# One plain fp32 matmul for each product of a decoder trunk, in place of three fp32r matmuls on split operands

## The chip, the cores and the metric

The kernel runs on one core of one Trainium2 chip. The metric is device time in microseconds (us), median over several executions. The kernel before takes 1388.41 us (three runs, 1388.27 to 1388.46). The engines are named as in the profile: PE (TensorE, matmuls), PEld (its weight loads, which have a row of their own), DVE (VectorE), ACT (ScalarE), POOL (GpSimd) and SP (SyncE, which issues nearly all DMAs here). PE takes one operand as weights (stationary, 128 columns) and streams the other through (the moving operand, up to 512 columns); sums over several matmuls build up in a PSUM bank. L159 means line 159 of the kernel before.

## The reference

The computation is a two-layer causal decoder trunk in float32 on 512 tokens of width 1024, with 256 memory tokens. Cut to what matters:

```python
for l in range(DEPTH):                                    # DEPTH = 2
    h = rmsnorm(x, norm_mix_g[l])
    if l % 2 == 0:
        x = x + pool_conv_mixer(h, ...)                   # 1024 -> 1536, pooling + conv, 1024 -> 1024
    else:
        x = x + mla_attention(h, ...)                     # 16 heads, low-rank q (384) and kv (256)
    x = x + memory_cross_attention(rmsnorm(x, ...), rmsnorm(mem, ...), ...)   # 4 heads of 256
    x = x + conv_ffn(rmsnorm(x, ...), ...)
return rmsnorm(x, final_norm_g)

def conv_ffn(h, w_up, conv_w, conv_b, w_down):
    a, g = jnp.split(h @ w_up, 2, axis=-1)                # 1024 -> 2 x 2816
    g = causal_dwconv(g, conv_w) + conv_b                 # 3 taps
    return (jax.nn.silu(g) * a) @ w_down                  # 2816 -> 1024
```

Nearly all arithmetic is in dense products of 128x128 weight tiles with 512 tokens.

## The kernel before, in words

Activations lie transposed, features on the 128 partitions and the 512 tokens along the free axis. So `x` is 8 tiles of 128x512, an MLP product has 22 such tiles, and one product is a 128x128 weight tile times a 128x512 activation tile.

**Split operands.** Each float32 operand is cut into a high part in the type fp32r and a low part that holds the rest (also fp32r). `load_w` (L147) brings a weight tile of up to 128x1024 by DMA into one of four raw buffers (`wr`), casts it on ACT into `wh` (L152) and forms `wl` as the difference on DVE (L153), with raised priority. Activations are split wherever they are made: `Norm.split` (L259, `hh` and `hl`), `split_psum` (L186), `split_sb` (L193), and by hand for the pooled outputs (L654), the latent queries (L925) and the memory tokens (`memory_gain`). `mm3` (L156) then makes a product from three fp32r matmuls into the same PSUM bank: high by high (L157), high by low (L158 or L159), low by high.

**Stages, in program order.** The mixer of layer 0: 12 output tiles of the input projection over 8 tiles of `h`; the first (`opening`, L621) runs while the tiles of `x` arrive; then the depthwise convolution, 31 taps, most of them as DVE operations (L677) interleaved with the keys and values of the memory tokens for both layers (`memory_kv`, L331); then the output projection. The keys for layer 0 (`K_NATIVE`, L340) were already plain fp32 matmuls on raw weights, with a moving operand of 256 columns. Cross-attention (L376): four heads, scores and values by `mm3`, softmax on DVE and ACT. MLP (`ffn`, L466): 44 output tiles of the up projection, gate and convolution on DVE and ACT, then the down projection. The 22 product tiles are taken in groups of 8, 8 and 6 (`FFN_GROUPS`): as soon as a group is there, its part of all 8 output tiles is summed in PSUM and added to `x` on DVE (L514); the last group goes through `residual` (L288), which also feeds the next norm. Layer 1 has latent attention (L889) in place of the mixer; its scores, transposes and values (L1016, L1041, L1053) are plain fp32 matmuls in both kernels, and so are the transposes of the norms, five taps of the convolution (L688) and one mean (L705). The last group of layer 1 is in `finale` (L517): 256 tokens at a time, so that the final norm of the first half runs beside the second.

**What orders the work.** Every engine runs its own instructions in a fixed order, and semaphores join them. The order is made when the kernel is built: a scheduler goes by the order of the program text and may put an instruction earlier where its inputs are there (`tc.high_priority` moves the splits of the weights ahead by 40 places; ACT's diagonal matrices of L687 run during the opening). Where the text interleaves (taps, `filler`, heads of the latent attention with a lag of 2) it was written so by hand. All weight loads go through SP's queue in program order, and a load waits until its raw buffer is free; before, that is when `wl` has been formed. All activations live in a pool of `SLOTS` = 58 tiles of 128x512, and PSUM has 8 banks.

```python
def mm3(ps, ah, al, bh, bl, first, last):
    pe.matmul(ps, ah, bh, start=first, stop=False)
    pe.matmul(ps, ah, bl, start=False, stop=False)
    pe.matmul(ps, al, bh, start=False, stop=last)
```

Of the kernel before, what the change touches and what calls it, by code (L numbers as in the profile page):

```python
# [12 lines left out]
F32R = mybir.dt.float32r  # L13
# [6 lines left out]
P = 128  # L20
# [30 lines left out]
SLOTS = 58  # L51
AHEAD = 40
FIN_AHEAD = 2
K_NATIVE = (True, False)
# [8 lines left out]
FFN_GROUPS = (8, 8, 6)  # L63

# columns of the packed per-channel constants
# [16 lines left out]
def _split_2pi():  # L82
    """2*pi*512 and 2*pi cut into parts whose products with the counts below are exact in float32."""
    def head(v, bits):
        m, e = math.frexp(v)
        return math.ldexp(math.floor(m * 2 ** bits), e - bits)

    big = 2.0 * math.pi * 512.0
    parts = []
    rest = big  # L90
    for _ in range(3):
        h = head(rest, 11)
        parts.append(h)
        rest -= h
    parts.append(rest)
    d1 = head(2.0 * math.pi, 13)
    return parts, (d1, 2.0 * math.pi - d1)
# [3 lines left out]
def kernel(ctx: ExitStack, tc: tile.TileContext, a):  # L101
# [24 lines left out]
    def f(t):  # L126
        return t.bitcast(F32)

# [13 lines left out]
    def load_raw(src, n):  # L142
        raw = wp.tile([P, WCOLS], F32, tag="wr", name=uid("wr"), bufs=4)
        sp.dma_start(raw[:, :n], src)
        return raw

    def load_w(src, n):  # L147
        raw = load_raw(src, n)
        hi = wp.tile([P, WCOLS], F32R, tag="wh", name=uid("wh"), bufs=3)
        lo = wp.tile([P, WCOLS], F32R, tag="wl", name=uid("wl"), bufs=3)  # L150
        with tc.high_priority(offset=AHEAD):
            act.copy(hi[:, :n], raw[:, :n])  # L152
            vec.tensor_tensor(lo[:, :n], raw[:, :n], f(hi[:, :n]), ALU.subtract)  # L153
        return hi, lo

    def mm3(ps, ah, al, bh, bl, first, last):  # L156
        pe.matmul(ps, ah, bh, start=first, stop=False)  # L157
        pe.matmul(ps, ah, bl, start=False, stop=False)  # L158
        pe.matmul(ps, al, bh, start=False, stop=last)  # L159
# [33 lines left out]
    def split_sb(src, name, shape=(P, T)):  # L193
        h = slot(name + "h", F32R, shape)
        l = slot(name + "l", F32R, shape)
        act.copy(h, src)
        vec.tensor_tensor(l, src, f(h), ALU.subtract)  # L197
        return h, l

    def newton_rsqrt(v, n, name):  # L200
        """1/sqrt(v) of a narrow tile."""
# [13 lines left out]
    def col_sums(acc, n=TB):  # L215
        """sums over the partitions of acc, tokens on partitions: [128, n]."""
# [7 lines left out]
    def row_rate(src, n, name):  # L224
        """1/rms of tokens whose features lie along the free axis: [128, n]"""
# [16 lines left out]
    def spread(r, n=TB, name="rb", out=None):  # L242
        """[128, n] with tokens on partitions -> [128, n * 128] with tokens along the free axis."""
# [7 lines left out]
    class Norm:  # L251
        """h = x * gain as hi and lo parts and the running sum of squares, tile by tile."""
# [6 lines left out]
        def split(self, k):  # L259
            if self.gain is not None:  # L260
                g = col(self.gain, self.base + k)
                h = slot("hh", F32R)
                l = slot("hl", F32R)
                act.activation(h, x[k], AF.Identity, scale=g)  # L264
                vec.scalar_tensor_tensor(l, x[k], g, f(h), ALU.mult, ALU.subtract)  # L265
                self.h.append((h, l))
# [36 lines left out]
    class Memory:  # L303
        """the memory tokens, normalised, in two stages"""
# [11 lines left out]
    def memory_gain(layer, memn, mg, mh):  # L316
        for i in range(KD // 2):
            m = slot("mg", shape=(P, 2, MEM))
            h = slot("mh", F32R, (P, 2, MEM))
            l = slot("ml", F32R, (P, 2, MEM))  # L320
# [3 lines left out]
            act.copy(h, m)  # L324
            vec.tensor_tensor(l, m, f(h), ALU.subtract)
            for j in range(2):
                mg.append(m[:, j, :])
                mh.append((h[:, j, :], l[:, j, :]))
            yield

    def memory_kv(layer, mg, mh, keep, native, kt, vt):  # L331
        """keys [d, mem] per head and values [mem, d]; keep takes each out of PSUM; a step per weight tile"""
        for hd in range(HX):
            ps = bank("kx", (P, 2, MEM))
            for j in range(2):
                src = a["xa_wk"][layer, 2 * hd + j]
                if native:
                    w = load_raw(src, D)
                    for k in range(KD):
                        pe.matmul(ps[:, j, :], w[:, k * P:(k + 1) * P], mg[k], start=k == 0, stop=k == KD - 1)  # L340
                else:
                    Linear(src, KD, ps[:, j, :]).run(mh, 0, KD)
                yield
            kt.append(keep(ps, (P, 2, MEM)))
        for half in range(2):
            ps = [bank("vx") for _ in range(MB)]
            for kk in range(KD // 2):
                wh, wl = load_w(a["xa_wv"][layer, half, kk], 2 * T)
                for j in range(2):
                    k = 2 * kk + j  # L350
                    c = slice(j * T, (j + 1) * T)
                    for m in range(MB):
                        h, l = mh[k]
                        s = slice(m * P, (m + 1) * P)
                        mm3(ps[m], h[:, s], l[:, s], wh[:, c], wl[:, c], k == 0, k == KD - 1)
                yield
            for m in range(MB):
                vt[m].append(keep(ps[m], (P, T)))

    def keep_slot(ps, shape):  # L360
        t = slot("kv0", F32, shape)
# [3 lines left out]
    def keep_whole(ps, shape):  # L365
        t = sl.tile(list(shape), F32, tag="kv1", name=uid("kv1"), bufs=8)
        act.copy(t, ps)
        return t

    def split_kv(kv):  # L370
        kt, vt = kv
        return ([split_sb(t, "k", (P, 2, MEM)) for t in kt],
                [[split_sb(t, "v") for t in row] for row in vt])

# [1 line left out]
    def cross_attention(layer, norm, kv, nxt):  # L376
# [4 lines left out]
        def project(hd, j):  # L381
# [3 lines left out]
            q.setdefault(hd, []).append(split_psum(lin.run(norm.h, KD // 2, KD), "q"))  # L385
            yield

        def scores(hd):
            kh, kl = kt[hd]
            mx = small("xmx", [P, TB])  # L390
            sc = []
            for u in range(2):
                ps = bank("sx", (P, 2, MEM))
                for b in range(2):
                    s = slice((2 * u + b) * P, (2 * u + b + 1) * P)
                    for j in range(2):
                        qh, ql = q[hd][j]
                        mm3(ps[:, b, :], qh[:, s], ql[:, s], kh[:, j, :], kl[:, j, :], j == 0, j == 1)
# [20 lines left out]
        def turn(hd):  # L419
            ptr[hd] = []  # L420
            for m in range(MB):
# [3 lines left out]
                ptr[hd].append(split_psum(pt, "pt"))  # L425

        def values(hd):
            for j in range(2):
                ps = bank("pv")
                c0 = (2 * hd + j) * P  # L430
                for m in range(MB):
                    vh, vl = vt[m][c0 // T]
                    c = slice(c0 % T, c0 % T + P)
                    mm3(ps, vh[:, c], vl[:, c], ptr[hd][m][0], ptr[hd][m][1], m == 0, m == MB - 1)
                o.append(split_psum(ps, "o"))
# [30 lines left out]
    def ffn(layer, norm, nxt, extra=None):  # L466
# [9 lines left out]
        def up(i):  # L476
# [15 lines left out]
            prod.append(split_sb(c, "f"))  # L492
# [3 lines left out]
        k0 = 0  # L496
        i = 0
        for n in FFN_GROUPS:
            k1 = k0 + n
            while i < min(k1 + 1, KF):  # L500
                if i == KF - 1 and nxt is None:
                    last = finale(layer, k0, k1 - k0)
                    next(last)
                up(i)
                i += 1
            if k1 == KF and nxt is None:
                last.send(prod[k0:k1])
                return
            for m in range(KD):
                ps = linear(a["ffn_down"][layer, m][:, k0 * P:k1 * P], prod[k0:k1])  # L510
                if k1 == KF:
                    residual(ps, m, nxt)
                else:
                    vec.tensor_tensor(x[m], x[m], ps, ALU.add)  # L514
            k0 = k1

    def finale(layer, k0, nk):  # L517
        """the last products, half of the tokens at a time, and the final norm of each half"""
        half = T // 2
        part = nk // 2  # L520
        w = []

        def weights(m):
            raw = load_raw(a["ffn_down"][layer, m][:, k0 * P:], nk * P)
            hi = [slot("dh", F32R, (P, part * P)) for _ in range(2)]
            lo = [slot("dl", F32R, (P, part * P)) for _ in range(2)]
            for q in range(2):
                c = slice(q * part * P, (q + 1) * part * P)
# [663 lines left out]
```

## Time and profile before

| | |
|---|---|
| median of the runs | 1388.41 us |
| span of the profiled execution | 1386.6 us |
| PE busy | 1371.6 us (99%), 6532 matmul records |
| PE weight loads busy | 1131.2 us (82%) |
| DVE busy | 889.0 us (64%) |
| ACT busy | 599.2 us (43%) |
| granted PE clock, mean | 0.999 |
| DMA | 135.28 MB, mean 98 GB/s |

The span counts from the first to the last instruction of the profiled execution; the timed median is 1.8 us above it. A matmul's record runs from its start to its modelled end, and records in a stream overlap, so the pace of a stream is read from the distance between starts and not from the length of one record. A plain fp32 product shows as two records with two weight loads: the 64 products of L340 stand as 128.

### The profile page before, as it was taken

Reading aid. Unit: us, or ns where it says so; the run is one execution under the profiler, and the core shown is the slowest. Engines: PE = TensorE matmul, PEld = TensorE weight load, DVE = VectorE, ACT = ScalarE, POOL = GpSimd, SP = SyncE. Lnnn points to the kernel's source line nnn. Section 1 sums busy time; section 2 is a strip of 40 time slices with the busy share of each in tenths; the row PEclk is TensorE's granted clock in tenths of the full one; section 3 lists DMA queues with packets and bytes.
Section 4 is the critical chain, followed back from the end, with each engine's and each line's share of the span. In section 5 each row is a group of like instructions: output and inputs, shape, how many; then the busy total and the mean of one; then the engine's idle time right before and its main releaser. Section 6 shows DMA issues by size and latency. Waiting matters only on the chain.

```text
span 1386.6 us, 16884 instructions
## 1 busy us (share of the span) xinstructions
PE 1371.6 (99%) x6532; PEld 1131.2 (82%) x6532; DVE 889.0 (64%) x1535; ACT 599.2 (43%) x976; POOL 6.3 (0%) x17
## 2 busy tenths in 40 slices
PE   8999999999999999999999999999999999999997
PEld 6888978888888888888887776888888888888887
DVE  6999988555685366445669775755566544653565
ACT  6416456443443143223447786644443322332343
POOL 0000000000000000000100000000000000000000
PEclk9999999999999999999999999999999999999999
DMA  9235524113333333333321111321223333233221
GB/s 331 93 106 188 169 91 145 61 56 98 108 97 91 105 93 93 104 91 87 97 83 50 43 46 46 107 76 61 76 91 96 102 92 106 91 93 106 84 84 62
DMA packets 42560, 135.28 MB, mean 98 GB/s; under 512 B 4848, under 2 KB 6512, under 8 KB 42480
## 3 DMA queue, kind: packets, MB, share of 16 engines
q1 hardware_dynamic: 41904, 133.45, 31.0%
q8 instruction: 51, 0.84, 0.2%
q10 hardware_dynamic: 576, 0.76, 0.2%
q14 instruction: 29, 0.24, 0.1%
HBM read 132.09 MB, written 2.10 MB: 97 GB/s over the span
## 4 chain that ended last, share of the span: by engine, by line
PE 90%; DVE 7%; ACT 2%; issue 1%; DMA 0%; SPq 0%; DVEq 0%; ACTq 0%
PE lin L159 24%; PE lin L157 24%; PE lin L158 24%; DVE cv L677 3%; PE s L1016 1%; PE mpv L1053 1%; DVE wl L153 1%; PE t L1041 1%; PE vx L158 1%; PE vx L159 1%; PE fin L157 1%; PE vx L157 1%; PE fin L158 1%; PE fin L159 1%; ACT p L1024 1%
## 5 line engine op out<-in xcount | busy, mean ns | idle before, releaser
L152 ACT CAST wh<-wr 128x1024 fp32r<-128x1024 f32 (+3 forms) x240 | 239.0, 998 | 485.0 <-PE lin L158 338.4
L157 PE MATMUL lin<-hh,wh 128*128 128x512 f32 x976 | 382.4, 392 | 5.9 <-ACT hh L264 5.9
L158 PE MATMUL lin<-hl,wh 128*128 128x512 f32 x976 | 381.1, 391 | 0.0
L159 PE MATMUL lin<-hh,wl 128*128 128x512 f32 x976 | 380.8, 390 | 0.2 <-DVE wl L153 0.2
L153 DVE TENSOR_TENSOR wl<-wr,wh 128x1024 fp32r<-128x1024 f32 (+3 forms) x240 | 276.9, 1155 | 60.4 <-ACT wh L152 58.9
L157 PEld LDWEIGHTS lin<-hh,wh 128*128 128x128 f32 x976 | 183.8, 188 | 43.2 <-ACT hh L264 5.9
L158 PEld LDWEIGHTS lin<-hl,wh 128*128 128x128 f32 x976 | 183.7, 188 | 39.4 <-DVE hl L265 2.1
L159 PEld LDWEIGHTS lin<-hh,wl 128*128 128x128 f32 x976 | 183.7, 188 | 38.7 <-DVE wl L153 0.7
L158 PE MATMUL lin<-fl,wh 128*128 128x512 f32 x304 | 118.4, 389 | 0.0
L159 PE MATMUL lin<-fh,wl 128*128 128x512 f32 x304 | 118.3, 389 | 0.0
L157 PE MATMUL lin<-fh,wh 128*128 128x512 f32 x304 | 118.1, 389 | 0.0
L514 DVE TENSOR_TENSOR x<-x,lin 128x512 f32<-128x512 f32 x32 | 22.0, 688 | 102.8 <-PE lin L159 102.8
L479 DVE TENSOR_TENSOR g<-lin,rb 128x512 f32<-128x512 f32 x44 | 30.4, 690 | 79.2 <-PE lin L159 79.2
L677 DVE SCALAR_TENSOR_TENSOR cv<-a,con,cv 128x509 f32<-128x509 f32 (+25 forms) x115 | 79.5, 728 | 0.1
L490 DVE TENSOR_TENSOR g<-lin,rb 128x512 f32<-128x512 f32 x44 | 30.4, 691 | 71.6 <-PE lin L159 71.4
L158 PEld LDWEIGHTS lin<-fl,wh 128*128 128x128 f32 x304 | 57.1, 188 | 12.1 <-DVE fl L197 0.2
L157 PEld LDWEIGHTS lin<-fh,wh 128*128 128x128 f32 x304 | 57.1, 188 | 11.8
L159 PEld LDWEIGHTS lin<-fh,wl 128*128 128x128 f32 x304 | 57.1, 188 | 11.7
L488 ACT ACTIVATE c<-c 128x512 f32<-128x512 f32 x44 | 27.8, 633 | 82.1 <-DVE c L487 82.1
L289 DVE TENSOR_TENSOR x<-x,lin 128x512 f32<-128x512 f32 x40 | 27.3, 686 | 35.6 <-PE lin L159 35.6
L158 PE MATMUL lin<-ol,wh 128*128 128x512 f32 x128 | 50.1, 391 | 0.0
L159 PE MATMUL lin<-oh,wl 128*128 128x512 f32 x128 | 49.9, 390 | 0.0
(351 smaller groups left out, 2062.4 us busy)
## 6 DMA issues: line engine op xcount, KB each, us to landing
wr<-in_ffn_up SPq DMA_DIRECT2D x88, 512.0 KB, 3.5
wr<-in_ffn_down SPq DMA_DIRECT2D x32, 512.0 KB, 3.5
wr<-in_xa_wk SPq DMA_DIRECT2D x16, 512.0 KB, 3.7
wr<-in_xa_wv SPq DMA_DIRECT2D x16, 512.0 KB, 4.2
wr<-in_xa_wq SPq DMA_DIRECT2D x16, 512.0 KB, 3.6
wr<-in_xa_wo SPq DMA_DIRECT2D x16, 512.0 KB, 3.5
wr<-in_ffn_down SPq DMA_DIRECT2D x16, 384.0 KB, 3.1
wr<-in_pc_in SPq DMA_DIRECT2D x11, 512.0 KB, 6.6
```

The source lines that it names most:

```text
L152: act.copy(hi[:, :n], raw[:, :n])
L153: vec.tensor_tensor(lo[:, :n], raw[:, :n], f(hi[:, :n]), ALU.subtract)
L157: pe.matmul(ps, ah, bh, start=first, stop=False)
L158: pe.matmul(ps, ah, bl, start=False, stop=False)
L159: pe.matmul(ps, al, bh, start=False, stop=last)
L289: vec.tensor_tensor(x[m], x[m], ps, ALU.add)
L479: vec.tensor_tensor(g, gps, rb, ALU.mult)
L488: act.activation(c, c, AF.Silu)
L490: vec.tensor_tensor(g, aps, rb, ALU.mult)
L514: vec.tensor_tensor(x[m], x[m], ps, ALU.add)
L677: vec.scalar_tensor_tensor(cv[i][:, s:], gl[i][:, :T - s], w, cv[i][:, s:], ALU.mult, ALU.add)
L1016: pe.matmul(ps[i], q[:, i * P:(i + 1) * P], k[:, :P * (i + 1)], start=True, stop=True)
```

## The change

Each product becomes one plain fp32 matmul on the operands as they are. `mm3`, `split_psum`, `split_sb`, `split_kv` and all other splits go: no cast on ACT and no difference on DVE for the weights, and one tile in place of two for each activation. `load_w` is the DMA alone, now into ten buffers (`WBUFS`), and a buffer is free when its last matmul has read it. Where a split's high part also moved a result out of PSUM, one ACT copy (`keep`) or one ACT activation stays. The keys for layer 0 and the matmuls that were plain fp32 stay as they are. The down projection of the MLP in layer 0 becomes, for each of the 8 output tiles, one sum over 22 tiles after all 22 have been made, with one `residual` each. In layer 1 `finale` first sums the first 16 tiles for all 8 output tiles (8 additions to `x`), then the last 6 as before; its weights for these come straight into slots by two DMAs for each output tile. `SLOTS` goes from 58 to 50. Comments and docstrings are dropped.

```diff
-SLOTS = 58
-AHEAD = 40
+SLOTS = 50
+WBUFS = 10
...
     def load_w(src, n):
-        raw = load_raw(src, n)
-        hi = wp.tile([P, WCOLS], F32R, tag="wh", name=uid("wh"), bufs=3)
-        lo = wp.tile([P, WCOLS], F32R, tag="wl", name=uid("wl"), bufs=3)
-        with tc.high_priority(offset=AHEAD):
-            act.copy(hi[:, :n], raw[:, :n])
-            vec.tensor_tensor(lo[:, :n], raw[:, :n], f(hi[:, :n]), ALU.subtract)
-        return hi, lo
...
+        w = wp.tile([P, WCOLS], F32, tag="wr", name=uid("wr"), bufs=WBUFS)
+        sp.dma_start(w[:, :n], src)
+        return w
...
             for k in range(k0, k1):
-                hi, lo = self.load(k)
+                w = self.load(k)
                 c = slice(k % KD * P, (k % KD + 1) * P)
-                xh, xl = xs[k]
-                mm3(self.ps, hi[:, c], lo[:, c], xh, xl, k == 0, k == self.nk - 1)
+                pe.matmul(self.ps, w[:, c], xs[k], start=k == 0, stop=k == self.nk - 1)
             return self.ps
...
-    def split_psum(ps, name, shape=(P, T)):
-        h = slot(name + "h", F32R, shape)
-        l = slot(name + "l", F32R, shape)
-        act.copy(h, ps)
-        vec.tensor_tensor(l, ps, f(h), ALU.subtract)
-        return h, l
...
+    def keep(ps, name, shape=(P, T)):
+        t = slot(name, F32, shape)
+        act.copy(t, ps)
+        return t
...
         def split(self, k):
             if self.gain is not None:
-                g = col(self.gain, self.base + k)
-                h = slot("hh", F32R)
-                l = slot("hl", F32R)
-                act.activation(h, x[k], AF.Identity, scale=g)
-                vec.scalar_tensor_tensor(l, x[k], g, f(h), ALU.mult, ALU.subtract)
-                self.h.append((h, l))
+                h = slot("h")
+                act.activation(h, x[k], AF.Identity, scale=col(self.gain, self.base + k))
+                self.h.append(h)
...
             vec.tensor_tensor(c, c, g, ALU.mult)
-            prod.append(split_sb(c, "f"))
+            prod.append(c)
...
+        for i in range(KF):
+            up(i)
+        if nxt is None:
+            finale(layer, prod)
+            return
+        for m in range(KD):
+            residual(linear(a["ffn_down"][layer, m], prod), m, nxt)
...
         def weights(m):
...
+            hold = [slot("dw", F32, (P, part * P)) for _ in range(2)]
+            for q, t in enumerate(hold):
+                c = (k0 + q * part) * P
+                sp.dma_start(t, a["ffn_down"][layer, m][:, c:c + part * P])
+            w.append(hold)
...
+        for m in range(KD):
+            ps = linear(a["ffn_down"][layer, m][:, :k0 * P], prod[:k0])
+            vec.tensor_tensor(x[m], x[m], ps, ALU.add)
+            if m >= KD - FIN_AHEAD:
+                weights(len(w))
...
                 ps = bank("fin")[:, :half]
-                for k in range(nk):
-                    wc = slice(k % part * P, (k % part + 1) * P)
-                    mm3(ps, hi[k // part][:, wc], lo[k // part][:, wc], prod[k][0][:, c], prod[k][1][:, c],
-                        k == 0, k == nk - 1)
+                for k in range(k0, KF):
+                    q, i = divmod(k - k0, part)
+                    pe.matmul(ps, w[m][q][:, i * P:(i + 1) * P], prod[k][:, c], start=k == k0, stop=k == KF - 1)
```

More of the change, by code (lines that the diff above doesn't have):

```diff
@@ L62 @@
 LATE = (1, 4, 1, 3, 1, 4, 1)
-FFN_GROUPS = (8, 8, 6)
 _COLS = {}
@@ L323, in memory_gain, with memory_kv @@
                                scale=col("norm_mem_g", layer * KD + 2 * i + j))
-            act.copy(h, m)
-            vec.tensor_tensor(l, m, f(h), ALU.subtract)
-            for j in range(2):
                 mg.append(m[:, j, :])
-                mh.append((h[:, j, :], l[:, j, :]))
             yield
-    def memory_kv(layer, mg, mh, keep, native, kt, vt):
+    def memory_kv(layer, mg, hold, kt, vt):
         for hd in range(HX):
@@ L335, in memory_kv @@
             for j in range(2):
[L336 to L342, printed above, removed]
+                Linear(a["xa_wk"][layer, 2 * hd + j], KD, ps[:, j, :]).run(mg, 0, KD)
                 yield
-            kt.append(keep(ps, (P, 2, MEM)))
+            kt.append(hold(ps, (P, 2, MEM)))
         for half in range(2):
@@ L347, in memory_kv, with hold_slot, hold_kv @@
             for kk in range(KD // 2):
-                wh, wl = load_w(a["xa_wv"][layer, half, kk], 2 * T)
+                w = load_w(a["xa_wv"][layer, half, kk], 2 * T)
                 for j in range(2):
                     k = 2 * kk + j
-                    c = slice(j * T, (j + 1) * T)
                     for m in range(MB):
-                        h, l = mh[k]
-                        s = slice(m * P, (m + 1) * P)
-                        mm3(ps[m], h[:, s], l[:, s], wh[:, c], wl[:, c], k == 0, k == KD - 1)
+                        pe.matmul(ps[m], mg[k][:, m * P:(m + 1) * P], w[:, j * T:(j + 1) * T],
+                                  start=k == 0, stop=k == KD - 1)
                 yield
             for m in range(MB):
-                vt[m].append(keep(ps[m], (P, T)))
-    def keep_slot(ps, shape):
-        t = slot("kv0", F32, shape)
+                vt[m].append(hold(ps[m], (P, T)))
+    def hold_slot(ps, shape):
+        return keep(ps, "kv0", shape)
+    def hold_kv(ps, shape):
+        t = sl.tile(list(shape), F32, tag="kv", name=uid("kv"), bufs=8)
         act.copy(t, ps)
         return t
[L365 to L373, printed above, removed]
     def cross_attention(layer, norm, kv, nxt):
@@ L384, in project @@
             yield
-            q.setdefault(hd, []).append(split_psum(lin.run(norm.h, KD // 2, KD), "q"))
+            q.setdefault(hd, []).append(keep(lin.run(norm.h, KD // 2, KD), "q"))
             yield
         def scores(hd):
-            kh, kl = kt[hd]
             mx = small("xmx", [P, TB])
@@ L396, in scores @@
                     for j in range(2):
-                        qh, ql = q[hd][j]
-                        mm3(ps[:, b, :], qh[:, s], ql[:, s], kh[:, j, :], kl[:, j, :], j == 0, j == 1)
+                        pe.matmul(ps[:, b, :], q[hd][j][:, s], kt[hd][:, j, :], start=j == 0, stop=j == 1)
                 vec.reduce_max(mx[:, 2 * u:2 * u + 2], ps, axis=AX.X)
@@ L431, in values @@
                 for m in range(MB):
[L432 to L435, printed above, removed]
+                    pe.matmul(ps, vt[m][c0 // T][:, c0 % T:c0 % T + P], ptr[hd][m], start=m == 0, stop=m == MB - 1)
+                o.append(keep(ps, "o"))
         def out(m):
@@ L491, in up, with finale @@
             vec.tensor_tensor(c, c, g, ALU.mult)
-            prod.append(split_sb(c, "f"))
+            prod.append(c)
             if i == 2 and extra is not None:
                 extra()
[L496 to L517, printed above, removed]
+        for i in range(KF):
[5 more added lines that the diff above has]
+            residual(linear(a["ffn_down"][layer, m], prod), m, nxt)
+    def finale(layer, prod):
         half = T // 2
-        part = nk // 2
+        k0 = 2 * KD
+        part = (KF - k0) // 2
         w = []
         def weights(m):
[L524 to L528, printed above, removed]
-                act.copy(hi[q], raw[:, c])
-                vec.tensor_tensor(lo[q], raw[:, c], f(hi[q]), ALU.subtract)
-            w.append((hi, lo))
+            hold = [slot("dw", F32, (P, part * P)) for _ in range(2)]
[3 more added lines that the diff above has]
+            w.append(hold)
         def final_rate(acc):
@@ L574, in finale @@
         xg = []
-        for m in range(FIN_AHEAD):
-            weights(m)
-        prod = yield
+        for m in range(KD):
[3 more added lines that the diff above has]
+                weights(len(w))
         done = None
@@ L630, in opening @@
                 c = slice(k % half * P, (k % half + 1) * P)
-                mm3(ps, hi[:, c], lo[:, c], *norm.h[k], k == 0, k == KD - 1)
+                pe.matmul(ps, w[:, c], norm.h[k], start=k == 0, stop=k == KD - 1)
             return ps
@@ L652, in pooled @@
             c = slice(i * P, (i + 1) * P)
-            mm3(ps, wh[:, c], wl[:, c], *part, True, True)
-            yh = slot("yah", F32R)
-            yl = slot("yal", F32R)
-            g = col("pool_scale", i)
-            act.activation(yh, ps, AF.Identity, scale=g)
-            vec.scalar_tensor_tensor(yl, ps, g, f(yh), ALU.mult, ALU.subtract)
-            cat.append((yh, yl))
+            pe.matmul(ps, wpool[:, c], part, start=True, stop=True)
+            y = slot("ya")
+            act.activation(y, ps, AF.Identity, scale=col("pool_scale", i))
+            cat.append(y)
         def convolve():
@@ L721, in normalise @@
                 act.activation(cv[i], cv[i], AF.Silu, bias=col("conv_ln_b", i), scale=col("conv_ln_g", i))
-            yield
-            for i in range(CT):
-                cat.append(split_sb(cv[i], "yb"))
+                cat.append(cv[i])
         cv = [sl.tile([P, T], F32, tag="cv", name=uid("cv"), bufs=CT) for _ in range(CT)]
@@ L801, in filler @@
         def filler():
-            for _ in memory_kv(1, *scaled, keep_whole, K_NATIVE[1], *kv):
+            for _ in memory_kv(1, scaled, hold_kv, *kv):
                 yield 2
@@ L831, in mixer @@
             pass
-        out[0] = split_kv(out[0])
         for m in range(KD):
@@ L971, in contents @@
                     c = slice((i * nk + k) * P, (i * nk + k + 1) * P)
-                    mm3(ps, wh[:, c], wl[:, c], xs[k][0], xs[k][1], k == 0, k == nk - 1)
+                    pe.matmul(ps, w[:, c], xs[k], start=k == 0, stop=k == nk - 1)
                 r0, r1 = KIND[k0][0], KIND[k1][0]
@@ L997, in group_values @@
                         c = slice(512 + k * 256, 512 + (k + 1) * 256)
-                        mm3(ps[:, b, :], ckv[k][0][:, s], ckv[k][1][:, s], wh[:, c], wl[:, c],
-                            k == 0, k == KKV - 1)
+                        pe.matmul(ps[:, b, :], ckv[k][:, s], w[:, c], start=k == 0, stop=k == KKV - 1)
                 t = slot("v", F32, (P, 2, 4 * VH))
```

76 lines of the change are left out of this document (24 added, 52 removed).

## The prediction

> **What bounds the kernel now.** I read the page first, its engine lines and slices.
>
> ```profile
> span 1386.6 us, 16884 instructions
> PE 1371.6 (99%) x6532; PEld 1131.2 (82%) x6532; DVE 889.0 (64%) x1535; ACT 599.2 (43%) x976; POOL 6.3 (0%) x17
> PE   8999999999999999999999999999999999999997
> PEclk9999999999999999999999999999999999999999
> ```
>
> PE is busy for 1371.6 of 1386.6 us, in every slice but the first and the last, at a clock granted in full. Busy alone doesn't prove a bound, because records overlap and their ends are modelled. So I went on to the waits of PE, and to stretches where another engine might set the pace.
>
> ```profile
> PE lin L157 <- ACT hh L264: 5.9, 1, 5.9
> PE lin L159 <- DVE wl L153: 0.2, 1, 0.2
> ```
>
> ```profile
> 50.00:100.00 50.00, 50.00 (x219) 40.95 (x218) 50.00 (x96) 11.63 (x21) 0.00 (x0) 1.00 0.29 89
> 400.00:500.00 100.00, 100.00 (x442) 82.82 (x442) 50.90 (x61) 29.60 (x35) 0.00 (x0) 1.00 0.32 95
> 742.00:848.00 106.00, 105.11 (x568) 75.19 (x568) 83.14 (x266) 82.98 (x196) 0.00 (x0) 1.00 0.18 55
> 1350.00:1386.60 36.60, 29.14 (x245) 28.77 (x243) 20.19 (x56) 13.74 (x32) 0.00 (x0) 0.94 0.19 65
> ```
>
> (Columns of the windows: busy time of PE, PEld, DVE, ACT and POOL with their instruction counts, then granted clock, DMA share, GB/s.) PE waits 5.9 us for its first operand and hardly at all after that. In the convolution (50 to 100 us) DVE is full as well, but PE doesn't fall idle beside it; in the MLP (400 to 500) DVE has half its time free; the latent attention (742 to 848) costs PE 0.9 us of idle. The kernel is bound by PE throughout, so the question is what one product costs PE before and after. What goes from DVE and ACT was on nobody's path.
>
> **The pace of three fp32r matmuls.** The timeline of PE in layer 0's MLP and norms gives the start of every matmul; here are the first and the last of 39, all of one kind.
>
> ```profile
> 699.84 0.39 PE L157 MATMUL lin<-hh,wh 128*128 128x512 f32 x1
> ...
> 708.45 0.39 PE L159 MATMUL lin<-hh,wl 128*128 128x512 f32 x1
> ```
>
> 38 steps in 8.61 us: 0.2266 us each, so a product of 512 columns takes 3 x 0.2266 = 0.680 us. With 256 columns, in the last stage (33 records, 32 steps, in 3.84 us):
>
> ```profile
> 1345.05 0.28 PE L159 MATMUL fin<-fh,dl 128*128 128x256 f32 x1
> ...
> 1348.89 0.28 PE L158 MATMUL fin<-fl,dh 128*128 128x256 f32 x1
> ```
>
> 0.120 us each, 0.360 us a product.
>
> **The pace of one plain fp32 matmul.** The kernel has this kind already: 64 products in the keys of layer 0 with 256 columns (128 records, so a product is two), and a few with 512.
>
> ```profile
> 81.67 2.75 PE L340 MATMUL kx<-mg,wr 128*128 128x256 f32 x12
> ```
>
> ```profile
> 180.11 0.86 PE mean L705 x2
> 784.30 2.16 PE s L1016 x8
> ```
>
> ```profile
> L340 PE MATMUL kx<-mg,wr 128*128 128x256 f32 x128 | 28.3, 379 | 0.0
> L1016 PE MATMUL s<-kA,qA 96*128 96x512 f32 x8 | 4.1, 592 | 0.0
> L1016 PE MATMUL s<-kA,qA 96*128 96x256 f32 x8 | 2.4, 379 | 0.0
> ```
>
> The first fence is the timeline, the second the chain of waits, the third groups by shape (busy us, then mean ns of one record). A run of 12 key records spans 2.75 us, the last of them 0.379 long, so 11 steps take 2.371: 0.2155 each, 0.431 us a product of 256 columns, against 0.360 for three fp32r. From 256 to 512 columns a record grows by 592 - 379 = 213 ns. The key record's step of 215.5 ns is thus 213 for its columns and 2.5 fixed, and a 512-column record should step by 426 + 2.5 = 428.5 ns, a product by 0.857 us. Bounds: nothing fixed, 0.852; twice the key product, 0.862. The chain agrees: the mean's two records take 0.86, and a head's eight score records (128, 256, 384 and 512 columns, two each) 2.16, which is 1.69 ns a column or 0.864 for 512. No row shows 512-column products in a long stream; I take 0.857, since the key stream shows the same two-record form held over many products.
>
> So the two-record product is dearer than the three-record one: 0.857 against 0.680. The Trainium skill's "FP8 and Floating Point Precision" (TensorE Precision Notes) speaks against the change too: true fp32 takes four passes through the array. With four times the isolated gap of about 216 ns that "TensorE: Matmul & The Clock Gate" (Back-to-back issue gap) gives for 512 columns, a product would be 0.864 and the added time, as an estimate from these pages, some 11 us more than my sum has. The key stream, 0.431 for 256 columns, agrees with four passes; its own step decides.
>
> **How many products.** The groups by shape give the fp32r records of one of the three lines:
>
> ```profile
> L158 PE MATMUL lin<-hl,wh 128*128 128x512 f32 x976 | 381.1, 391 | 0.0
> L158 PE MATMUL lin<-fl,wh 128*128 128x512 f32 x304 | 118.4, 389 | 0.0
> L158 PE MATMUL lin<-ol,wh 128*128 128x512 f32 x128 | 50.1, 391 | 0.0
> L158 PE MATMUL lin<-mol,wh 128*128 128x512 f32 x64 | 24.9, 390 | 0.0
> L158 PE MATMUL vx<-wl,mh 128*128 128x512 f32 x64 | 25.1, 393 | 0.1
> L158 PE MATMUL fin<-fl,dh 128*128 128x256 f32 x96 | 27.1, 283 | 0.0
> L158 PE MATMUL kx<-ml,wh 128*128 128x256 f32 x64 | 18.1, 283 | 0.0
> L158 PE MATMUL sx<-kl,qh 128*128 128x256 f32 x64 | 18.0, 283 | 0.0
> ```
>
> The 512-column rows make 1536. The loops add 64 (second half of the mixer's output projection and first, 32 each), 32 values of the cross-attention, 24 + 16 contents and 12 rotary queries of the latent attention, and 4 pooled: 1688 in all. The 256-column rows make 224, and the values of the latent attention's heads 32 more: 256. Check: 3 x 1944 = 5832 of the 6532 records, and the rest are the plain ones.
>
> **The sum for PE.** 1688 x (0.857 - 0.680) = 298.8 us and 256 x (0.431 - 0.360) = 18.2 us: +317.0 us, all on the path that sets the end. With 0.852 it would be 308.5, with 0.862 it would be 325.4. PE records fall to 6532 - 1944 = 4588.
>
> **What goes from DVE and ACT, and from PE's small stalls.**
>
> ```profile
> L152 ACT CAST wh<-wr 128x1024 fp32r<-128x1024 f32 (+3 forms) x240 | 239.0, 998 | 485.0 <-PE lin L158 338.4 <-issue 107.8 <-PE vx L159 14.9
> L153 DVE TENSOR_TENSOR wl<-wr,wh 128x1024 fp32r<-128x1024 f32 (+3 forms) x240 | 276.9, 1155 | 60.4 <-ACT wh L152 58.9 <-PE st L219 1.5
> L157 PE MATMUL lin<-cqh,wh 128*128 128x512 f32 x12 | 6.0, 500 | 0.0
> ```
>
> The two weight splits alone take 239.0 us from ACT and 276.9 from DVE, and the activation splits more. They are hidden behind PE now and are worth nothing there; uncovered, they would have been visible as waits of PE, which the rows above put at 0.2 us. What PE can get back are delays inside its busy records: the 12 high-part records of the rotary queries last 500 ns where the groups above last 389 to 393, 1.3 us in all, because a low part is late. At the start there is a little more:
>
> ```profile
> 5.94 0.79 PE L157 MATMUL lin<-hh,wh 128*128 128x512 f32 x1 [5.94 <-ACT hh L264]
> ...
> 10.31 0.41 PE L157 MATMUL lin<-hh,wh 128*128 128x512 f32 x1
> ...
> 14.58 0.40 PE L157 MATMUL lin<-hh,wh 128*128 128x512 f32 x1
> ```
>
> The opening's 24 records take 8.64 us from 5.94 to 14.58, where 24 x 0.2266 = 5.44 would do: the first nine take 4.37 up to 10.31, 0.49 each or about half pace, and after that they wait for each low part. Eight plain products at half pace up to 10.31 and 0.857 after that take some 9.0, so the opening grows by about 0.4 and not by the 1.4 that the sum holds. With a stall of the kind of the rotary queries in a few other places of the attention I take 4 us back in all; the bounds are 0 and 8. The tail, from the last matmul on, stays: the same final norm, the same transposes. The MLP's 22-tile sum has the same matmuls as its three groups. In layer 0 it takes 16 additions from DVE, which has the time to spare; for the last of 22 tiles PE has 21 products, 18 us, to do before it is needed. The ten weight buffers need no faster DMA: a 512 KB tile lands in about 3.5 us by the page and will feed PE for 8 x 0.857 = 6.9 us.
>
> ```profile
> wr<-in_ffn_up SPq DMA_DIRECT2D x88, 512.0 KB, 3.5
> ```
>
> **Sum.** Span 1386.6 + 317.0 - 4 = 1699.6; the median of the runs lies 1.8 us above the profiled span (1388.4 against 1386.6), which gives 1701.4: 1701.
>
> **Rivals.** *(a) Weight loads set the pace (the other side: faster).* PEld is busy 82% of the time, and a product goes from three loads to two. If each record waited for its load, a product would be 2 x 0.2266 = 0.453 for 512 columns and 2 x 0.120 for 256, saving 382.5 + 30.7 us: about 975 us. It decides as soon as a 512-column plain record steps by less than 0.34 us (half of 0.680). Against it: the 256-column fp32r records above step by 0.120, less than the 0.19 of a load, so loads overlap one another; and the mean's and scores' rows. 3%. The Trainium skill's "Perfetto Trace Analysis" (Identifying the Most-Contended Engine) says to judge PE's headroom by the share of weight loads and not by matmul busy time; by that rule 82% would leave loads as the suspect, and the trace doesn't bear it out.
>
> *(b) The clock.* If four-pass products made the chip grant less clock, all of PE's 1689 us of work would stretch. At 0.94, the lowest of the windows above, it is 6% more, 108 us: about 1810. It decides from 0.99 on, where 17 us fill the range. Against it: in the stretches with plain fp32 (50 to 100 and 742 to 848) the clock is 1.00, and the 0.94 belongs to the tail with PE mostly idle. 4%.
>
> *(c) A new wait at the start or in the slots.* Ten buffers let SP issue six more weight tiles, 3.1 MB, beside the loads that the first norm needs.
>
> ```profile
> GB/s 331 93 106 188 169 91 145 61 56 98 108 97 91 105 93 93 104 91 87 97 83 50 43 46 46 107 76 61 76 91 96 102 92 106 91 93 106 84 84 62
> ```
>
> At the first slice's 331 GB/s they take 9.3 us. If PE's transposes for the row factor came that much later, or 50 slots held it up as long somewhere, the time would be about 1711. For it: DMA is fullest there. Against it: SP issues in order, the norm's loads come before those tiles, and slots hold one tile in place of two. 6%.
>
> *(d) The change costs nothing* (a four-pass product hidden as it is): nothing in the rows allows it. 1%, 1388.
>
> **How the numbers follow.** The forecast, 1701 us, has 86%. Its own range is the price's (-8.5, +8.4) and the give-back's (-4, +4), at most 1689 to 1713 when both ends fall together. Few times will lie at the lower corner, so I start at 1690; (c) lies inside, and a little above it the range ends, at 1716. (a), (b) and (d) are left out, 8% in all. Below 0.2% a difference can't be told from none here. Faster 3% (a), same 1% (d), slower 96%.
>
> **What would show it.** Plain 512-column records should step by 0.4285 us, 256-column ones by 0.2155; PE has 4588 records and stays at 98 or 99%; DVE falls below a third of the span and ACT to about a fifth (the weight splits, the activation splits and 24 additions gone from rows of 889 and 599 us); the granted clock stays at 0.99 or above. The forecast is wrong if 512-column products in a stream step otherwise than in the mean's two records, if PE shows waits of more than 10 us beyond the first, or if the clock drops.

## The result, and the profile after

The changed kernel takes 1699.49 us (median of four runs, 1698.99 to 1700.16) against 1388.37 us: a ratio of 1.224, with a 95% interval of 1.2223 to 1.2258. That is 311 us more. The forecast was 1701 us.

From the page of the changed kernel: its span, engines, slices, and the chain of work that ended last.

```profile
span 1697.4 us, 11929 instructions
PE 1683.0 (99%) x4588; PEld 827.5 (49%) x4588; DVE 490.5 (29%) x1066; ACT 321.3 (19%) x642; POOL 5.9 (0%) x17
...
PE   8999999999999999999999999999999999999998
...
PEclk9999999999999999999999999999999999999999
...
PE 99%; DMA 0%; ACT 0%; DVE 0%; DVEq 0%; issue 0%; SPq 0%; ACTq 0%
```

PE has 4588 records in place of 6532, almost a third fewer, and is busy for 311 us longer. DVE lost 398.5 us of work, ACT 277.9, the weight loads 303.7, and hardly any of it shows in the time (some 8 us, taken up below): the chain is PE alone for 99% of the span. Fewer instructions, less work on three engines and a longer time fit together only if one instruction of the busiest engine got dearer. Two pieces of the chain in order of time (start, length, both in us), and the matmuls by shape (busy us, mean ns of one record), show the price:

```profile
423.44 453.20 PE lin L159 x1056
...
1645.94 23.31 PE fin L518 x108
```

```profile
L159 PE MATMUL lin<-h,wr 128*128 128x512 f32 x1936 | 835.6, 592 | 0.0
...
L159 PE MATMUL lin<-cq,wr 128*128 128x512 f32 x24 | 11.0, 592 | 0.0
L557 PE MATMUL lin<-h,wr 128*128 128x512 f32 x16 | 9.8, 782 | 6.9 <-ACT h L232 6.9
```

In the MLP of layer 0, 1056 records of 512 columns follow one another without a break in 453.20 us, 0.429 us each: 0.858 us a product, where three fp32r matmuls took 0.680. The last stage's 256-column records step by 23.31 / 108 = 0.216. The rotary queries' records last the same 592 ns as all others. The opening's records (L557) still last longer: the first six step by 0.853 us, twice 0.429, up to 12.2 us.

### The profile page after: what moved, and what is told of

It reads as the page before. It is cut to its first block, busy times and chain, and to the rows that moved or that the text cites. A ratio compares the mean times of both kernels' runs of the same rounds, so it can differ in the third digit from the quotient of the medians.

```text
span 1697.4 us, 11929 instructions
## 1 busy us (share of the span) xinstructions
PE 1683.0 (99%) x4588; PEld 827.5 (49%) x4588; DVE 490.5 (29%) x1066; ACT 321.3 (19%) x642; POOL 5.9 (0%) x17
## 4 chain that ended last, share of the span: by engine, by line
PE 99%; DMA 0%; ACT 0%; DVE 0%; DVEq 0%; issue 0%; SPq 0%; ACTq 0%
PE lin L159 78%; PE kx L159 3%; PE vx L307 3%; PE fin L518 2%; PE s L930 2%; PE nope L888 2%; PE sx L342 2%; PE pv L376 2%; PE t L955 1%; PE mpv L967 1%; PE v L913 1%; PE lin L557 1%; PE xpt L368 0%; PE st L189 0%; PE tap L611 0%; DMA x<-in_xT 0%
## 5 line engine op out<-in xcount | busy, mean ns | idle before, releaser
L159 PE MATMUL lin<-h,wr 128*128 128x512 f32 x1936 | 835.6, 592 | 0.0
L159 PEld LDWEIGHTS lin<-h,wr 128*128 128x128 f32 x1936 | 366.5, 190 | 452.3 <-issue 451.5
L159 PE MATMUL lin<-c,wr 128*128 128x512 f32 x608 | 261.3, 592 | 0.0
L159 PEld LDWEIGHTS lin<-c,wr 128*128 128x128 f32 x608 | 115.5, 190 | 145.4 <-issue 145.4
L159 PE MATMUL lin<-o,wr 128*128 128x512 f32 x256 | 111.0, 593 | 0.0
L600 DVE SCALAR_TENSOR_TENSOR cv<-a,con,cv 128x509 f32<-128x509 f32 (+29 forms) x115 | 77.9, 725 | 0.2
L159 PE MATMUL kx<-mg,wr 128*128 128x256 f32 x256 | 56.1, 379 | 0.0
L307 PE MATMUL vx<-wr,mg 128*128 128x512 f32 x128 | 55.9, 592 | 0.0
L159 PE MATMUL lin<-mo,wr 128*128 128x512 f32 x128 | 55.7, 593 | 0.0
L159 PEld LDWEIGHTS kx<-mg,wr 128*128 128x128 f32 x256 | 48.6, 190 | 8.6 <-issue 2.2
```

The lines of the kernel that those rows point to most:

```text
L159: pe.matmul(self.ps, w[:, c], xs[k], start=k == 0, stop=k == self.nk - 1)
L307: pe.matmul(ps[m], mg[k][:, m * P:(m + 1) * P], w[:, j * T:(j + 1) * T], start=k == 0, stop=k == KD - 1)
L600: vec.scalar_tensor_tensor(cv[i][:, s:], gl[i][:, :T - s], w, cv[i][:, s:], ALU.mult, ALU.add)
```

## The experiments

All runs below were timed beside the kernel before. The first of them is the changed kernel itself, run again as the base of the next three.

**The base.**

> The changed kernel itself, as the base for the other runs beside it. Both theories: 1699.5 us within 0.1%, ratio to the kernel before 1.222 to 1.226.

1698.98 us, ratio 1.2235 (1.2217 to 1.2254). It lies 0.5 us from the first time, and the next three are compared with it.

**The MLP's down projection in three groups again.**

```diff
-        for m in range(KD):
-            residual(linear(a["ffn_down"][layer, m], prod), m, nxt)
+        for n in (8, 8, 6):
+            ...                                   # up projection as far as the group needs
+            for m in range(KD):
+                ps = linear(a["ffn_down"][layer, m][:, k0 * P:k1 * P], prod[k0:k1])
+                ...                               # x[m] += ps, or residual for the last group
```

> The changed kernel with the MLP's down projection in groups of 8, 8 and 6 tiles again, all products plain fp32. Theory (only PE's pace counts; the 22-tile sum has the same matmuls as its groups): 1699 us, within 2 us of the changed kernel; DVE busy goes up by about 16 us (24 additions of 0.69 us) with no wait of PE. Rival (the one sum of 22 tiles is itself a gain or a loss, by additions or by a PSUM bank held for 19 us): a difference of more than 4 us either way.

1699.37 us, 0.4 from the base. The engines' line of its page:

```profile
PE 1682.7 (99%) x4588; PEld 827.5 (49%) x4588; DVE 507.2 (30%) x1090; ACT 321.0 (19%) x642; POOL 5.9 (0%) x17
```

24 instructions and 16.7 us more on DVE, none of it in the time. The part of the change about the 22-tile sum is worth nothing either way here, so the difference has to come from the rest of the change.

**The weight splits put back beside plain products.**

```diff
-        w = wp.tile([P, WCOLS], F32, tag="wr", name=uid("wr"), bufs=WBUFS)
-        sp.dma_start(w[:, :n], src)
-        return w
+        raw = wp.tile([P, WCOLS], F32, tag="wr", name=uid("wr"), bufs=4)
+        sp.dma_start(raw[:, :n], src)
+        ...                                       # hi, lo: 3 buffers each
+            act.copy(hi[:, :n], raw[:, :n])
+            vec.tensor_tensor(lo[:, :n], raw[:, :n], hi[:, :n], ALU.subtract)
+        return hi
```

> The changed kernel with the weight splits put back on ACT and DVE (cast and difference for each weight tile, 4 raw and 3 plus 3 split buffers); the plain fp32 products read the cast copy, the difference is read by nobody. Theory (PE covers that work, and only single late tiles cost it anything): ACT rises by about 239 us and DVE by about 277 us of busy time, the time stays at 1699 to 1705 us. Rival (the removed work was worth more than the 9 us by which PE's stalls shrank, so that putting it back costs as much): over 1708 us.

1698.73 us: no difference from the base (1698.98). The engines' line of its page, and PE's waits:

```profile
PE 1682.8 (99%) x4588; PEld 827.3 (49%) x4588; DVE 761.4 (45%) x1314; ACT 555.3 (33%) x890; POOL 5.9 (0%) x17
```

```profile
PE lin L562 <- ACT h L237: 6.0, 1, 6.0
PE s L935 <- ACT qA L895: 0.4, 1, 0.4
```

DVE works 270.9 us more than in the changed kernel and ACT 234.0, and PE waits 0.4 us more for ACT in one place. Behind PE at this pace the splits of the weights are free, and four raw with three cast buffers do as well as ten; taking the splits away paid for none of the dearer products. The run doesn't show what the small stalls of the kernel before were made of: PE takes longer for each weight tile here, and no product reads the low part.

**The same columns with twice the weight loads.**

```diff
-                pe.matmul(self.ps, w[:, c], xs[k], start=k == 0, stop=k == self.nk - 1)
+                n = xs[k].shape[-1]
+                for u in range(n // 256):
+                    s = slice(u * 256, (u + 1) * 256)
+                    pe.matmul(self.ps[:, s], w[:, c], xs[k][:, s], ...)
```

> The changed kernel with each 512-column product of the Linear helper (1540 of them) cut into two of 256 columns: as many columns through the array, twice the weight loads. Theory (columns times passes set the pace, plus some 2.5 ns for each record): a product takes 4 x 0.216 = 0.864 in place of 0.858 us, +9 us, 1706 to 1712 us, PEld near 85% busy. Rival (weight loads set the pace, at 0.227 us for each, as the fp32r stream would have it): 4 x 0.227 = 0.907 us a product, +75 us, about 1775 us.

1707.63 us, 8.7 above the base, where 9 were expected and 75 for loads that set the pace. Its span, engines' line, and the largest group by shape:

```profile
span 1705.8 us, 18146 instructions
...
PE 1690.3 (99%) x7668; PEld 1412.6 (83%) x7668; DVE 490.6 (29%) x1066; ACT 321.4 (19%) x642; POOL 5.9 (0%) x17
```

```profile
L162 PE MATMUL lin<-h,wr 128*128 128x256 f32 x3872 | 840.5, 379 | 0.0
```

The loads' busy time grows by 585 us, to about the share it had in the kernel before (82%), and the time by what 3080 further records cost at 2.8 ns each. In these plain products the loads lie beside the matmuls, and the columns streamed set the pace. The Trainium skill's "Perfetto Trace Analysis" (Identifying the Most-Contended Engine) reads PE's headroom from this share, next to the share of the peak arithmetic rate; here 49% and 83% stand for the same bound and times 0.5% apart, so the share alone doesn't measure the headroom.

**Two fp32r matmuls for each product, and one.** From the kernel before, with all splits left in (the edit of the first run; the second keeps only the first matmul, with `stop=last`):

```diff
     pe.matmul(ps, ah, bh, start=first, stop=False)
-    pe.matmul(ps, ah, bl, start=False, stop=False)
-    pe.matmul(ps, al, bh, start=False, stop=last)
+    pe.matmul(ps, ah, bl, start=False, stop=last)
```

> The kernel before with two fp32r matmuls for each product (the third, low part of the first operand by high part of the second, is left out of the sum; all splits stay). Theory (a product costs its passes, and DVE's 889 us are free only while PE takes longer): PE's work falls by 1688 x 0.2266 + 256 x 0.120 = 413 us, which would be 975 us; but in the first 250 us DVE has work for nearly all of the time, so the mixer can't shrink with PE: 1020 to 1080 us, DVE over 80% busy. Rival (the splits are free whatever PE does): 975 us.

> The kernel before with one fp32r matmul for each product (only high part by high part is summed; all splits stay, the low parts are read by nobody). Theory: PE's work alone would allow about 562 us; DVE, 889 us busy before, now sets the pace nearly everywhere: 890 to 1000 us, DVE over 90% busy. Rival (PE's passes alone count): 562 to 620 us.

1091.75 us with two, ratio 0.7863 (0.7848 to 0.7879); 1052.82 with one, ratio 0.7583 (0.7568 to 0.7598). The engines' lines and granted clocks of the two pages, two first, and of the second PE's longest waits:

```profile
PE 1003.7 (92%) x4588; PEld 799.1 (73%) x4588; DVE 876.2 (80%) x1535; ACT 596.6 (55%) x976; POOL 6.3 (1%) x17
...
PEclk9899987979999999999999999899989999999999
```

```profile
PE 710.8 (68%) x2644; PEld 510.1 (48%) x2644; DVE 868.5 (83%) x1535; ACT 593.1 (56%) x976; POOL 5.8 (1%) x17
...
PEclk9699666867779568879676888897788896986957
```

```profile
PE lin L157 <- ACT hh L262: 54.6, 31, 6.2
PE lin L157 <- DVE g L488: 43.8, 16, 5.0
PE lin L157 <- ACT fh L194: 38.7, 12, 5.0
```

The first matmul taken away brought 297 us of the 413 that its passes cost; the second brought 39. So the splits were free only because PE took longer, which is what both expectations said, and the rival (975 and 562 to 620 us) is out. Both times lie above the ranges expected, by 12 and 53 us. What was missed is in the pages: with one matmul DVE is not over 90% busy but 83%, and the waits show PE standing still for ACT and for DVE in turn. The granted clock is lower too, a mean of 0.96 and of 0.796; the last section shows what a wait does to the matmuls behind it.

**The change made, and undone, on one part alone.** In the kernel before, the memory keys' 64 products of 256 columns in layer 0 were plain, those of layer 1 split:

```diff
-K_NATIVE = (True, False)
+K_NATIVE = (False, False)      # all keys split
+K_NATIVE = (True, True)        # the other run: all keys plain
```

> The kernel before with the memory keys of layer 1 as plain fp32 too (64 products of 256 columns): the change made on one part alone. Theory (0.431 against 0.360 us a product): +4.5 us, 1393 us. Rival (8 weight tiles less to split where DVE is full give back as much as PE loses): 1388 to 1390 us.

> The kernel before with the memory keys of layer 0 (64 products of 256 columns) also as three fp32r matmuls on split weights, in place of plain fp32: the change undone where the kernel before had it already. Theory (PE's pace decides as long as DVE keeps up): 64 x (0.431 - 0.360) = -4.5 us, 1384 us. Rival (DVE is full from 50 to 150 us and gets 8 more weight tiles of 1.16 us to split, 9 us, of which PE sees a part): no gain or a loss, 1388 to 1394 us.

All keys plain: 1392.61 us against 1388.44, ratio 1.0035 (1.0023 to 1.0046), +4.2 us where the price difference of 0.071 us on 64 products says 4.5. Here a small part of the change shows the same price as the whole, and the rival, that fewer splits give as much back, is out.

All keys split: 1397.13 us, ratio 1.0063 (1.0048 to 1.0078), +8.7 us. The theory that PE's pace decides, -4.5 us, falls here, and its rival was too mild. PE's waits, and 150 to 200 us by window (PE, PEld, DVE, ACT and POOL busy, granted clock, DMA share, GB/s) in that kernel:

```profile
PE mean L705 <- DVE lacc L700: 8.0, 1, 8.0
```

```profile
150.00:200.00 50.00, 41.93 (x191) 33.68 (x190) 46.85 (x71) 16.79 (x23) 0.00 (x0) 0.90 0.36 115
```

PE waits for the end of the convolution, which DVE had hidden before with little to spare. In the kernel before, DVE ends the sum over the channels (`lacc`) at 176.0 us, and PE gets to the mean, which reads it, at 180.0. With all keys split DVE ends it at 187.4, 11 us later, while PE is there by 179.5. So the mean starts 7.6 us later than before, slower matmuls behind the wait bring that to 9.7 (the last section shows them), a little comes back later, and the span grows from 1386.6 to 1395.7 us. DVE's busy time rises from 889.0 to 898.2; that these 9.2 us and the span's 9.1 are nearly equal is a coincidence. What PE saves on the keys is lost in the wait. The page of the kernel before had a sign of this, a chain that isn't all PE:

```profile
PE 90%; DVE 7%; ACT 2%; issue 1%; DMA 0%; SPq 0%; DVEq 0%; ACTq 0%
```

So the two layers' keys differ: in layer 0 plain products cost PE 4.5 us more and keep DVE's splits off the path, which gains 8.7 us against split keys; in layer 1 they cost the 4 us and spare nothing that counts.

**One fp32r matmul and no splits.** The two runs with fewer matmuls pointed to a kernel without the low parts altogether. The main lines of the edit; the low parts of the activations and the plain keys of layer 0 go too, and the cast weights have six buffers in place of three:

```diff
-            vec.tensor_tensor(lo[:, :n], raw[:, :n], f(hi[:, :n]), ALU.subtract)
-        return hi, lo
+        return hi, hi
...
-    pe.matmul(ps, ah, bh, start=first, stop=False)
-    pe.matmul(ps, ah, bl, start=False, stop=False)
-    pe.matmul(ps, al, bh, start=False, stop=last)
+    pe.matmul(ps, ah, bh, start=first, stop=last)
```

> One fp32r matmul for each product and no low parts at all: nothing is subtracted, weights are cast on ACT alone, the memory keys of layer 0 too, results go straight to fp32r. The low parts of both operands are left out of every product of the dense layers, so the products have fp32r's precision. Theory (each product costs its passes, and what bounds the kernel then is the next engine): PE's work is about 514 us, ACT's about 575, DVE's about 475 with the mixer's convolution in one piece; 640 to 760 us. Rival (PE still sets the end): 540 to 560 us.

> As the run with high parts only, but after the mixer every second weight tile is cast on DVE. The same parts of the products are left out. Theory (ACT and DVE both stand between the weights and PE): 20 to 60 us less than with ACT alone, 600 to 720 us. Rival (ACT is not what binds): no difference, within 5 us.

754.11 us, ratio 0.5421 (0.5402 to 0.5439), and 760.55, ratio 0.5478 (0.5467 to 0.5488). This beats both kernels by far, at the price of what it leaves out: it isn't the same computation but one at fp32r's precision. The first lies in its range, near the upper end. Its engines' line and chain:

```profile
PE 593.6 (79%) x2580; PEld 444.3 (59%) x2580; DVE 493.9 (66%) x1090; ACT 556.4 (74%) x932; POOL 5.8 (1%) x17
...
DVE 32%; PE 29%; ACT 26%; DMA 7%; issue 4%; SPq 0%; DVEq 0%; ACTq 0%
```

PE no longer sets the end (540 to 560 us is out): three engines share the chain. PE is busy for 593.6 us where 514 were expected, at a mean granted clock of 0.91. The second expectation missed, and so, by a little, did its rival. Casting half of the later weights on DVE takes 83 us from ACT, adds 52 to DVE and costs 6 us; DVE's share of the chain rises from 32% to 40%. With the chain spread over three engines, moving work from one to another gained nothing.

## Why the prediction was right

**The bound.** PE busy for 99%, in full clock, with one wait of 5.9 us: that reading held. The two runs with added DVE and ACT work behind plain products (three groups, splits put back) moved the time by at most 0.4 us.

**The price.** It rested on 64 plain products of 256 columns and a handful of 512, since no long stream of the latter was there. The step from the difference of record lengths (213 ns for 256 columns, 2.5 fixed) said 0.4285 us; the stream has 0.429. The run with halved columns puts the fixed part at 2.8 ns. The Trainium skill's "FP8 and Floating Point Precision" (TensorE Precision Notes) has four passes for true fp32: the trace agrees, 0.858 us being four times 0.2145; the page estimate of 0.864 lay 0.006 above it. That loads don't set this price, and that it holds product by product, is shown by the halved columns and by the keys of layer 1.

**The count and the sum.** 4588 records came, as predicted. At the measured steps the products cost 1688 x (0.858 - 0.680) + 256 x (0.432 - 0.360) = 300.5 + 18.4 = 318.9 us, where the prediction had 317.0.

**What PE gets back.** This is the term that was mis-sized, and one reading behind it was wrong. The span grew by 1697.4 - 1386.6 = 310.8 us, so 8.1 came back in place of 4, just past the stated bound of 8. Adding up, over neighbouring matmuls of a trace, how far their starts lie apart beyond the pace of their kind gives 12.9 us of small stalls before and 4.8 after: 8.1 less. Two smaller terms nearly cancel: the first operand, which the prediction let come as before, came 1.0 us later (PE's first wait 6.9 against 5.9), and the latent attention's values, matmuls of 64 columns that the sum leaves out, took 1.7 us less.

By place, the stalls of PE's first 16 us fall from about 3.7 to 2.8, those between plain matmuls (mostly the scores, transposes and values of the attentions) from about 4.6 to 2.0, and some 4 us inside and right behind the split products are gone. The opening grew by 1.0 us (8.64 to 9.65), not by 0.4: its half pace lasted up to 12.2 us, where the prediction had it end at 10.3. The rotary queries gave nothing back. The prediction took their 500 ns for a low part that is late, but the last of these low parts (`cql`) is written at 729.9 us, and the three long records start at 755.0, 785.9 and 816.5. Each of them starts 0.03 us after the start of a plain score matmul and lasts 0.8 us, with the end of that matmul in it; the other nine last 0.4 to 0.5. How much of the rest was owed to low parts that came late isn't settled.

So the forecast came out 2 us from the time with a price 1.9 us too low in the sum and a give-back 4 us too small. The two errors cancel in part, and that part is luck; the price and the count, which make nearly all of the 311 us, are not.

**The rivals.** (a), loads that set the pace, is out by the halved columns. (b): the clock stayed at 0.999. (c): no new wait of PE in the slots or behind the ten buffers; the waits of PE in the changed kernel are a single line:

```profile
PE lin L557 <- ACT h L232: 6.9, 1, 6.9
```

What the prediction didn't see is how thin the cover was in the mixer. It said that uncovered splits would have shown as waits of PE, 0.2 us. That is right for the kernel as it stood, but DVE was only 3.9 us ahead there, and the run with all keys split shows that the next 9 us of DVE work put PE 8 us into a wait.

## What to carry to other kernels

Count what one instruction of the bounding engine costs in start-to-start steps before counting instructions: a product in fewer records can be the dearer one. Work taken from an engine that stays hidden behind the bound is worth next to nothing, however much of it there is (here 676 us went, and at most 8 of it shows in the time), but ask of each stage how much more that engine could take, since in a stage with two nearly full engines a small addition becomes a wait. Here a price that the trace shows in one shape carried over to another, by cutting its step into a part for each column and a fixed one. And a record that is long isn't yet a stall: look at where the one before it starts.

## What was not expected of the hardware

**A table load that moved onto the path.** ACT's first instruction is preceded by a load of its function table, 1.28 us. The timelines of the kernel before and of the changed one:

```profile
1.67 1.28 ACT L152 ACT_TABLE_LOAD   x1 [1.67 <-PEq L1181]
3.85 0.62 ACT L152 CAST wh<-wr 128x512 fp32r<-128x512 f32 x1 [0.90 <-DMA wr<-in_pc_in]
5.17 0.72 ACT L264 ACTIVATE hh<-x,con 128x512 fp32r<-128x512 f32 x1 [0.71 <-DMA x<-in_xT]
```

```profile
4.86 1.28 ACT L232 ACT_TABLE_LOAD   x1 [4.86 <-DMA x<-in_xT]
6.15 1.33 ACT L232 ACTIVATE h<-x,con 128x512 f32<-128x512 f32 x2
```

Before, it ran while ACT had nothing to do, ahead of the first weight cast. With the cast gone, it stands behind the wait for `x`, and PE's first product starts 1 us later. With the weight casts put back, PE's first wait is 6.0 us again. The size varies, since `x` itself lands at different times: in the four traces without the cast the load starts at 4.9 to 6.0 us and PE at 6.9 to 8.1.

**Idle PE makes the next matmuls dear.** In the run with all keys split, PE is idle for 8 us before the mean, and the mean's two records (of one tile: shortest, median and longest, ns) last about twice what they did in the kernel before, whose line stands second:

```profile
L705 PE MATMUL mean<-lacc,om x2: 1057/1124/1191, 187.5 to 188.5; 128*128 128x512 f32 x2
```

```profile
L705 PE MATMUL mean<-lacc,om x2: 590/590/591, 180.0 to 180.4; 128*128 128x512 f32 x2
```

The granted clock of that window is 0.90, and 0.796 on average in the run with one matmul, where PE waits often. The Trainium skill's "TensorE: Matmul & The Clock Gate" (Part 1, The HAM clock gate) says that PE falls to half its clock after about 3.4 us of idling; the doubled records after 8 us agree. The fp32r matmuls behind the mean also step by 0.43 us in place of 0.227, up to 191.9 us, and PE's lag behind the kernel before grows there from 7.6 to 9.7 us. So this wait cost more than its length, which the expectations for the two runs with fewer matmuls had left out.
